# Attention's transfers between tiles issued from GpSimd's queue, in a two-layer decoder trunk on one core

## The chip, the cores and the metric

The kernel runs on one core of a Trainium2 chip. The metric is device microseconds of one execution. The engines are named as in the profile: PE is TensorE, PEld its weight loads, DVE VectorE, ACT ScalarE, POOL GpSimd, SP SyncE. Each of them works through its own list of instructions in order, and a transfer (DMA) is issued by an instruction in the list of one of them.

## The reference

The program computes a trunk of two layers for 512 tokens of width 1024, ahead of which 16 learned tokens are put (528 in all). Layer 0 is attention with a forget gate, layer 1 a gated linear recurrence; each is followed by a gated MLP with a short convolution. The change lies in the attention:

```
xn = rms_norm(h, norm_g)
q, k, v, f_logit, o_gate = split(xn @ w_in)            # 16 heads of 64
q = rms_norm(q, q_gain) * hd ** -0.5;  k = rms_norm(k, k_gain)
c = cumsum(log_sigmoid(f_logit + b_f))                 # per head
s = q . k + c[query] - c[key], -inf above the diagonal
o = softmax(s) @ v
h = h + (o * sigmoid(o_gate)) @ w_out
```

## The kernel before, in words

The whole trunk is one program, a chain of stages: setup, attention (`fox`), MLP, recurrence (`hgrn`), MLP. Activations lie transposed, 128 channels by 528 tokens, and are worked on in two halves of 264. Matrix products are computed to near float32 by splitting each operand into a high and a low part (`xhi`/`xlo`, `hi`/`lo`) and adding three products: these are the lines L263, L266 and L267, the projections, and L312 for the values. Weights come from DRAM by SP's queue into `raw`; ACT rounds them to `hi` (L210) and DVE makes `lo` (L126).

Attention goes by eight pairs of heads `p` in a software pipeline. One step of the loop runs for different pairs at once:

- `stage_a(p+3)`: the projections of q and k (L263 to L267), their squares on ACT (L545) and the scaled copy (L546). A product with `hsel` (L554) gives the sums of squares in `strow`; four transfers (L559) lay them out as `am2`, DVE takes the inverse root, and two transfers (L569) bring it back as `rows`.
- `stage_n(p+2)`: a product with `rows` (L583) spreads the factors over the partitions, DVE multiplies (L584), ACT rounds to `stg` (L588), and `pack` sends the high and low parts by six transfers per pair (L610) into `pk`, the operand tiles of one head. There are six such tiles, `pk_245` to `pk_270`, used in turn.
- `stage_l(p+1)`: four transfers per pair (L619) put the forget gate's cumulative sums `cneg` into the operand tile. Then `lse` finds the logarithm of each query's sum of exponentials for each head: scores by L726, L727 and, on the diagonal, L729; DVE reduces to the maximum `negm` (L739, L745); ACT takes exponentials with their sum (L119, to `junk`, with an accumulator read) and a logarithm (`ls`); DVE splits it (`lr`, L757, L126); a transposition by TensorE (L760) and a DVE copy (L762) give the row `lrow`, and three transfers (L765, L766) write it into the operand tile.
- `stage_t(p)`: `attend` computes the scores again, transposed and now with that row in the contraction (L782, L783; mask L785), ACT takes exponentials `pt` (L119), and L797 multiplies with the values.

The output projection at the end reads tiles that were operands before (`pk_265`, `pk_270` as its high and low part). The first MLP's weights are partly formed by transfers that add: SP brings one summand, POOL issues a transfer that accumulates the other (L232).

The pieces are written in an order that `weave` sets by costs in the code, and the program is then scheduled by the tile framework, which simulates a timeline and from that sets the order of each engine's list:

```
        for p in range(-3, NPAIR):
            ...
            weave(
                (chain(*fill), 0.97 * cost),
                (stage_n(p + 2) if 0 <= p + 2 < NPAIR else None, 1.0),
                (stage_l(p + 1) if 0 <= p + 1 < NPAIR else None, 4.3),
                (stage_t(p) if p >= 0 else None, 8.5),
                (stage_f() if p == -2 else None, 3.5),
            )
```

Which engine issues a transfer is chosen in the code; where it stands in that engine's list, and in which order TensorE takes projections and scores, follows from the simulated timeline. PSUM has two banks for projections (`psp`), four for scores (`pss`), one for attention's output (`psc`) and one for sums and factors (`psd`).

Of the kernel before, what the change touches and what calls it, by code (L numbers as in the profile page):

```python
# [12 lines left out]
F32 = mybir.dt.float32  # L13
# [69 lines left out]
class Builder:  # L83
# [297 lines left out]
    def fox(self, ctx):  # L381
        nc, tc, a = self.nc, self.tc, self.a
# [38 lines left out]
        def bank():  # L421
            return self.bank("p")
# [96 lines left out]
        def stage_a(p):  # L519

            raw = {}
            sqs = []
            blocks = []
            for w_ in range(2):
                wt = self.weights(a["wqk"][p, w_], KT) if p else self.first[w_]
                banks = [self.bank(b) for b in ("pp", "cd")[w_]] if p == 0 else None
                blocks.append((wt, banks))
                if p == 0 and w_ == 1:
                    units = [
                        self.proj_unit(ps[:, :tn], [wt], self.x, t0, tn)  # L530
                        for wt, banks in blocks
                        for ps, (t0, tn) in zip(banks, full)
                    ]
                    for step in zip(*units):
                        yield sum(step)
            for w_, nm in ((0, "q"), (1, "k")):
                wt, banks = blocks[w_]
                sq = (s2 if w_ else self.sqp).tile([P, T], F32, name="sqq", tag="sqk" if w_ else "sq", bufs=2 - w_)
                rw = s2.tile([P, T], F32, name="raw" + nm, tag="raw" + nm)
                g = qg if nm == "q" else self.vcol(V_KG)  # L540
                for i, (t0, tn) in enumerate(full):
                    ps = banks[i] if banks else bank()
                    if not banks:
                        yield from self.proj_unit(ps[:, :tn], [wt], self.x, t0, tn)
                    nc.scalar.square(sq[:, t0 : t0 + tn], ps[:, :tn])  # L545
                    nc.scalar.activation(rw[:, t0 : t0 + tn], ps[:, :tn], AF.Copy, scale=g)  # L546
                sqs.append(sq)
                raw[nm] = rw

            strow = s2.tile([P, 264], F32, name="strow", tag="strow", bufs=1)  # L550
            pst = self.bank("d")
            for g in range(4):
                t0, tn = full[g % 2]
                mm(pst[32 * g : 32 * g + 32, :tn], hsel, sqs[g // 2][:, t0 : t0 + tn], start=True, stop=True)  # L554
            nc.scalar.copy(strow, pst[:, :264])
            yield 0.9
            am2 = self.tiny.tile([64, 33], F32, name="am2", tag="am2")
            for g in range(4):
                nc.sync.dma_start(  # L559
                    am2[16 * g : 16 * g + 16, :], strow[32 * g : 32 * g + 2, :].rearrange("r (j c) -> r j c", c=33)  # L560
                )
            nc.vector.tensor_tensor(am2, am2, et, ALU.add)
            y = self.rsqrt(am2, "q")
            yr = self.tiny.tile([64, 2, 33], F32R, name="yr", tag="yr")
            nc.vector.tensor_copy(yr[:, 0, :], y)
            self.sub(yr[:, 1, :], y, yr[:, 0, :].bitcast(F32))
            rows = rowbufs[p % 2]
            for x in range(2):
                nc.sync.dma_start(  # L569
                    rows[8 * x : 8 * x + 8, :].rearrange("r (j c) -> r j c", c=33).bitcast(F32),  # L570
                    yr[:, x, :].bitcast(F32),
                )
            scaled[p] = raw, rows
# [29 lines left out]
        def pack(p, stg):  # L603
            packs[p] = []
            for hd in range(2):
                head = 2 * p + hd
                d = slots[head % NSLOT]
                packs[p].append(d)
                sl = slice(64 * hd, 64 * hd + 64)
                dma = lambda o, i: nc.sync.dma_start(o.bitcast(F32), i.bitcast(F32))  # L610
                dma(d["pk"][0:64, 0:2, :], stg[sl, 0:3:2, :])
                dma(d["pk"][0:64, 2:4, :], stg[sl, 0:4:3, :])
                dma(d["pk"][64:128, 2:4, :], stg[sl, 1:3, :])

        def stage_l(p):
            for hd, d in enumerate(packs[p]):
                head = 2 * p + hd
                for x in range(2):
                    nc.sync.dma_start(  # L619
                        d["k1"][64 + x : 65 + x, :].rearrange("x (j c) -> x j c", c=CW).bitcast(F32),  # L620
                        cneg[8 * head : 8 * head + 8, x, :].bitcast(F32),
                    )
            for d in packs[p]:
                yield from self.lse(d, s2, identb, maskq)
# [42 lines left out]
        for p in range(-3, NPAIR):  # L667
# [4 lines left out]
            if p + 3 < NPAIR:  # L672
                fill.append(stage_a(p + 3))
                cost += 12.8
# [6 lines left out]
            if p == NPAIR - 1:  # L681
# [3 lines left out]
# [5 lines that stand above are left out]
# [4 lines left out]
            while gated and p >= max(gated[0], 5 + gated[0] // 4):  # L694
                m = gated.pop(0)
                o = gate[:, m, :]
# [15 lines left out]
    def lse(self, d, s2, identb, maskq):  # L712

        nc = self.nc
        mm = nc.tensor.matmul
        q1, k1, q2, k2 = d["q1"], d["k1"], d["q2"], d["k2"]
        negm = self.tiny.tile([P, 6], F32, name="negm", tag="negm")
        ssum = self.tiny.tile([P, 6], F32, name="ssum", tag="ssum")
        nc.gpsimd.memset(negm, 0.0)
        nc.gpsimd.memset(ssum, 1.0)  # L720

        def score(i, qs, qn, c0, c1):
            ps = self.bank("s")
            o = ps[:qn, : c1 - c0]
            diag = c1 > qs
            mm(o, q1[0:66, qs : qs + qn], k1[0:66, c0:c1], start=True, stop=False)  # L726
            mm(o, q2[:, qs : qs + qn], k2[:, c0:c1], start=False, stop=not diag)  # L727
            if diag:
                mm(ps[:qn, qs - c0 : qs - c0 + qn], identb[:qn, :qn], maskq[:qn, :qn], start=False, stop=True)  # L729
            return o  # L730

        def expsum(o, qn, col, src):
            junk = s2.tile([P, 400], BF16, name="junk", tag="junk")
            self.act(junk[:qn, : o.shape[1]], o, AF.Exp, bias=negm[:qn, col : col + 1], accum_out=ssum[:qn, src : src + 1])

        for i in range(4):
            qs, qn = QT[i]
            o = score(i, qs, qn, 0, qs + qn)
            nc.vector.tensor_reduce(negm[:qn, i : i + 1], o, AX.X, ALU.max, negate=True)  # L739
            expsum(o, qn, i, i)  # L740
            yield 0.3
        qs, qn = QT[4]
        oa = score(4, qs, qn, 0, 264)
        ob = score(4, qs, qn, 264, 528)
        nc.vector.tensor_reduce(negm[:, 4:5], oa, AX.X, ALU.max, negate=True)  # L745
        nc.vector.tensor_reduce(negm[:, 5:6], ob, AX.X, ALU.max, negate=True)
        nc.vector.tensor_tensor(negm[:, 4:5], negm[:, 4:5], negm[:, 5:6], ALU.min)
        expsum(oa, qn, 4, 4)
        expsum(ob, qn, 4, 5)
        yield 0.6  # L750
        nc.vector.tensor_tensor(ssum[:, 4:5], ssum[:, 4:5], ssum[:, 5:6], ALU.add)
        ls = self.tiny.tile([P, 5], F32, name="ls", tag="ls")
        self.act(ls, ssum[:, 0:5], AF.Ln)
        self.sub(ls, negm[:, 0:5], ls)

        lr = self.tiny.tile([P, 10], F32R, name="lr", tag="lr")
        nc.vector.tensor_copy(lr[:, 0:5], ls)  # L757
        self.sub(lr[:, 5:10], ls, lr[:, 0:5].bitcast(F32))
        pr = self.bank("s")
        mm(pr[:10, :P], lr, self.identr, start=True, stop=True)  # L760
        lrow = self.tiny.tile([10, P], F32R, name="lrow", tag="lrow")
        nc.vector.tensor_copy(lrow, pr[:10, :P])  # L762
        for x in range(2):
            row = q1[96 + x : 97 + x, 16:].rearrange("x (i c) -> x i c", c=P)
            nc.sync.dma_start(row.bitcast(F32), lrow[5 * x + 1 : 5 * x + 5, :].bitcast(F32))  # L765
        nc.sync.dma_start(q1[96:98, 0:16].bitcast(F32), lrow[0:10:5, 0:16].bitcast(F32))  # L766
        yield 0.2

    def attend(self, o0, o1, p, ds, v, po, s2, maskk):
# [763 lines left out]
```

## Time and profile before

| | |
|---|---|
| median of 3 runs | 1461.14 us (1461.13 to 1461.83) |
| the profiled execution's own time | 1463.9 us |
| its span | 1462.0 us |
| mean granted clock of TensorE | 0.994 |
| TensorE busy | 1435.2 us, 98% |
| VectorE, ScalarE, GpSimd busy | 67%, 45%, 10% |
| transfers | 230.97 MB, mean 158 GB/s |

In the profile, "PE psp L263 <- ACT xhi L332" means that a matmul of line 263 into a tile psp waited for ScalarE's write of xhi at line 332. In an instruction's row, the first number is its start from the beginning of the span, the second its duration; a bracket holds how long the engine was idle before it and what ended that. Matmuls are pipelined, so a row's duration is longer than the step from one to the next.

### The profile page before, as it was taken

To read this page: it belongs to the slowest core of one execution; us is meant where nothing else is said; L and a number is where in the kernel's file an instruction comes from. 1 tells how busy PE (TensorE), PEld (TensorE's weight loads), DVE (VectorE), ACT (ScalarE), POOL (GpSimd) and SP (SyncE) were. 2 spreads that over 40 slices of the span, in tenths; PEclk is the share of its full clock that TensorE was granted. 3 is DMA by queue.
4 is the path that set the end of the run, shared out by engine and by line. 5 is a ranking of instruction groups with operands and counts; after the bars stand their busy time and mean duration, and the time that the engine had idled before them with its cause. 6 is when DMAs were issued, how large, how long until landed. Compare 5 with 4: busy or idle time off the path is not lost.

```text
span 1462.0 us, 29172 instructions
## 1 busy us (share of the span) xinstructions
PE 1435.2 (98%) x11482; PEld 1349.0 (92%) x11482; DVE 974.9 (67%) x2079; ACT 663.1 (45%) x1293; POOL 150.2 (10%) x265
## 2 busy tenths in 40 slices
PE   7999999999999999999999999999999999999998
PEld 6888888888999999999999999999999889999997
DVE  6555555774667675666785667587567777866773
ACT  5355555563434444333563224333345565544551
POOL 6000000001112100112001101011111110000000
PEclk9999999999999999999999999999999999999999
DMA  4433334435999884678737617374587795544542
GB/s 160 119 105 90 90 90 123 124 99 137 293 231 247 213 254 137 171 193 197 218 92 181 168 22 181 91 178 103 126 238 169 208 265 162 173 143 137 161 146 85
DMA packets 99696, 230.97 MB, mean 158 GB/s; under 512 B 13528, under 2 KB 15320, under 8 KB 99560
## 3 DMA queue, kind: packets, MB, share of 16 engines
q1 hardware_dynamic: 79400, 188.47, 40.3%
q0 software_dynamic: 20160, 40.64, 18.3%
q8 instruction: 90, 1.47, 0.4%
q14 instruction: 46, 0.38, 0.1%
HBM read 213.62 MB, written 75.24 MB: 198 GB/s over the span
## 4 chain that ended last, share of the span: by engine, by line
PE 91%; DMA 4%; DVE 2%; ACT 1%; issue 1%; SPq 1%; ACTq 0%; DVEq 0%
PE psp L263 9%; PE psp L267 9%; PE psp L266 9%; PE pss L263 8%; PE pss L267 8%; PE pss L266 8%; PE psp L312 5%; PE psc L797 2%; PE psp L1292 2%; PE psp L1290 2%; PE psp L1291 2%; PE psp L1184 1%; PE psp L1186 1%; PE psp L1185 1%; PE pss L951 1%; PE psd L1292 1%
## 5 line engine op out<-in xcount | busy, mean ns | idle before, releaser
L210 ACT CAST hi<-raw 128x1024 fp32r<-128x1024 f32 (+3 forms) x250 | 234.1, 939 | 381.3 <-PE psp L266 96.1
L126 DVE TENSOR_TENSOR lo<-raw,hi 128x1024 fp32r<-128x1024 f32 (+3 forms) x254 | 275.5, 1088 | 100.9 <-ACT hi L210 96.8
L263 PE MATMUL psp<-xhi,hi 128*128 128x264 f32 (+1 forms) x984 | 283.9, 290 | 6.1 <-ACT xhi L332 6.1
L266 PE MATMUL psp<-xlo,hi 128*128 128x264 f32 (+1 forms) x984 | 283.6, 288 | 3.2 <-DVE xlo L333 3.2
L267 PE MATMUL psp<-xhi,lo 128*128 128x264 f32 (+1 forms) x984 | 283.9, 289 | 0.0
L263 PEld LDWEIGHTS psp<-xhi,hi 128*128 128x128 f32 x984 | 186.8, 190 | 10.7 <-ACT xhi L332 6.1
L266 PEld LDWEIGHTS psp<-xlo,hi 128*128 128x128 f32 x984 | 187.1, 190 | 6.0 <-DVE xlo L333 3.7
L267 PEld LDWEIGHTS psp<-xhi,lo 128*128 128x128 f32 x984 | 187.0, 190 | 1.7 <-issue 1.6
L267 PE MATMUL pss<-xhi,lo 128*128 128x264 f32 (+3 forms) x520 | 149.8, 288 | 0.0
L263 PE MATMUL pss<-xhi,hi 128*128 128x264 f32 (+3 forms) x520 | 149.1, 287 | 0.0
L266 PE MATMUL pss<-xlo,hi 128*128 128x264 f32 (+3 forms) x520 | 149.1, 287 | 0.0
L232 POOL DMA_DIRECT2D s<-gu x80 | 66.4, 856 | 332.3 <-DMA s<-gu 300.9
L263 PEld LDWEIGHTS pss<-xhi,hi 128*128 128x128 f32 x520 | 97.8, 188 | 0.6
L267 PEld LDWEIGHTS pss<-xhi,lo 128*128 128x128 f32 x520 | 97.7, 188 | 0.7
L266 PEld LDWEIGHTS pss<-xlo,hi 128*128 128x128 f32 x520 | 97.7, 188 | 0.7
L263 PE MATMUL pss<-room,hi 128*128 128x512 f32 (+1 forms) x182 | 69.6, 387 | 1.7 <-ACT hi L210 1.7
L267 PE MATMUL pss<-room,lo 128*128 128x512 f32 (+1 forms) x182 | 70.4, 387 | 0.0
L266 PE MATMUL pss<-room,hi 128*128 128x512 f32 (+1 forms) x182 | 70.2, 386 | 0.0
L312 PE MATMUL psp<-hi,xhi 128*128 128x256 f32 x232 | 66.9, 288 | 2.5 <-ACT v L599 2.5
L1292 PE MATMUL psp<-xhi,lo 128*128 128x258 f32 x240 | 67.9, 283 | 0.9 <-DVE lo L126 0.8
L1157 ACT CAST hi<-left 128x768 fp32r<-128x768 f32 (+1 forms) x56 | 43.4, 781 | 54.0 <-PE psp L1185 18.3
L1290 PE MATMUL psp<-xhi,hi 128*128 128x258 f32 x240 | 67.6, 282 | 0.0
(488 smaller groups left out, 3798.1 us busy)
## 6 DMA issues: line engine op xcount, KB each, us to landing
raw<-gu SPq DMA_DIRECT2D x48, 512.0 KB
s<-gu SPq DMA_DIRECT2D x80, 256.0 KB
s<-gu POOLq DMA_DIRECT2D x80, 256.0 KB, 6.0
raw<-gu SPq DMA_DIRECT2D x60, 256.0 KB
pk<-stg SPq DMA_DIRECT2D x48, 264.0 KB
raw<-s SPq DMA_DIRECT2D x40, 256.0 KB
raw<-s SPq DMA_DIRECT2D x20, 512.0 KB
raw<-wqk SPq DMA_DIRECT2D x14, 512.0 KB
```

The costliest lines, as they stand in the source:

```text
L126: self.nc.vector.tensor_tensor(out, x, y, ALU.subtract)
L210: nc.scalar.copy(hi, raw)
L232: nc.gpsimd.dma_start(out, y, accum_op=ALU.add, max_dma_last_dim=4 * n)
L263: ins = mm(ps, hi[:, i, :], xh, start=k == 0, stop=False)
L266: mm(ps, hi[:, i, :], xl, start=False, stop=False)
L267: mm(ps, lo[:, i, :], xh, start=False, stop=k == total - 1)
L312: mm(ps[:tn, :256], y[:, t0 : t0 + tn], w, start=n == 0, stop=n == 23)
L797: ins = mm(o, v[:kn, j, 2 * (p % 2) + hd, :], w[hd][0], start=j == 0, stop=j == last)
L1157: nc.scalar.copy(hi, raw)
L1290: mm(ps, hi[:, k0 + k, :], xh, start=start and k == 0, stop=False, skip_group_check=not start)
L1291: mm(ps, hi[:, k0 + k, :], xl, start=False, stop=False, skip_group_check=not start)
L1292: mm(ps, lo[:, k0 + k, :], xh, start=False, stop=k == 3, skip_group_check=not start)
```

## The change

176 transfers of the attention are issued by GpSimd in place of SP: 32 of `am2` (L559), 16 of `rows` (L569), 48 of `pk` from `stg` (L610), 32 of `cneg` (L619) and 48 of `lrow` (L765, L766). The loads of weights, of the gate's `z` and of the residual stay on SP. The two memsets in `lse`, 32 in all, go from GpSimd to VectorE. Nothing is added or removed.

```diff
--- before.py
+++ after.py
@@ -556,7 +556,7 @@
             yield 0.9
             am2 = self.tiny.tile([64, 33], F32, name="am2", tag="am2")
             for g in range(4):
-                nc.sync.dma_start(
+                nc.gpsimd.dma_start(
                     am2[16 * g : 16 * g + 16, :], strow[32 * g : 32 * g + 2, :].rearrange("r (j c) -> r j c", c=33)
                 )
             nc.vector.tensor_tensor(am2, am2, et, ALU.add)
@@ -566,7 +566,7 @@
             self.sub(yr[:, 1, :], y, yr[:, 0, :].bitcast(F32))
             rows = rowbufs[p % 2]
             for x in range(2):
-                nc.sync.dma_start(
+                nc.gpsimd.dma_start(
                     rows[8 * x : 8 * x + 8, :].rearrange("r (j c) -> r j c", c=33).bitcast(F32),
                     yr[:, x, :].bitcast(F32),
                 )
@@ -607,7 +607,7 @@
                 d = slots[head % NSLOT]
                 packs[p].append(d)
                 sl = slice(64 * hd, 64 * hd + 64)
-                dma = lambda o, i: nc.sync.dma_start(o.bitcast(F32), i.bitcast(F32))
+                dma = lambda o, i: nc.gpsimd.dma_start(o.bitcast(F32), i.bitcast(F32))
                 dma(d["pk"][0:64, 0:2, :], stg[sl, 0:3:2, :])
                 dma(d["pk"][0:64, 2:4, :], stg[sl, 0:4:3, :])
                 dma(d["pk"][64:128, 2:4, :], stg[sl, 1:3, :])
@@ -616,7 +616,7 @@
             for hd, d in enumerate(packs[p]):
                 head = 2 * p + hd
                 for x in range(2):
-                    nc.sync.dma_start(
+                    nc.gpsimd.dma_start(
                         d["k1"][64 + x : 65 + x, :].rearrange("x (j c) -> x j c", c=CW).bitcast(F32),
                         cneg[8 * head : 8 * head + 8, x, :].bitcast(F32),
                     )
@@ -716,8 +716,8 @@
         q1, k1, q2, k2 = d["q1"], d["k1"], d["q2"], d["k2"]
         negm = self.tiny.tile([P, 6], F32, name="negm", tag="negm")
         ssum = self.tiny.tile([P, 6], F32, name="ssum", tag="ssum")
-        nc.gpsimd.memset(negm, 0.0)
-        nc.gpsimd.memset(ssum, 1.0)
+        nc.vector.memset(negm, 0.0)
+        nc.vector.memset(ssum, 1.0)
 
         def score(i, qs, qn, c0, c1):
             ps = self.bank("s")
@@ -762,8 +762,8 @@
         nc.vector.tensor_copy(lrow, pr[:10, :P])
         for x in range(2):
             row = q1[96 + x : 97 + x, 16:].rearrange("x (i c) -> x i c", c=P)
-            nc.sync.dma_start(row.bitcast(F32), lrow[5 * x + 1 : 5 * x + 5, :].bitcast(F32))
-        nc.sync.dma_start(q1[96:98, 0:16].bitcast(F32), lrow[0:10:5, 0:16].bitcast(F32))
+            nc.gpsimd.dma_start(row.bitcast(F32), lrow[5 * x + 1 : 5 * x + 5, :].bitcast(F32))
+        nc.gpsimd.dma_start(q1[96:98, 0:16].bitcast(F32), lrow[0:10:5, 0:16].bitcast(F32))
         yield 0.2
 
     def attend(self, o0, o1, p, ds, v, po, s2, maskk):
```

With other costs in the simulated timeline the scheduler writes the lists of the attention stage in another order; behind that stage they are as before. Three places follow.

The first is TensorE's list at the first pair of heads (`pk_245` holds head 0, `pk_250` head 1; `psp` rows are projections, `pss` rows with `pk` scores). TensorE's list before, round the first head's L760:

```order
L263 MATMUL psp<-xhi,hi 128x264
L266 MATMUL psp<-xlo,hi 128x264
L583 MATMUL psd<-rows_177,selr 128x264
L267 MATMUL psp<-xhi,lo 128x264
L263 MATMUL psp<-xhi,hi 128x264
L760 MATMUL pss<-identr,lr 10x128
L726 MATMUL pss<-pk_250 16x16
L727 MATMUL pss<-pk_250 16x16
```

TensorE's list after, from the last scores of head 0 to the first of head 1:

```order
L726 MATMUL pss<-pk_245 128x264
L727 MATMUL pss<-pk_245 128x264
L726 MATMUL pss<-pk_245 128x264
L727 MATMUL pss<-pk_245 128x264
L729 LDWEIGHTS identb
L729 MATMUL pss<-maskq,identb 128x128
L760 MATMUL pss<-identr,lr 10x128
L726 MATMUL pss<-pk_250 16x16
```

and further on in the same list, from the last scores of head 1:

```order
L729 LDWEIGHTS identb
L729 MATMUL pss<-maskq,identb 128x128
L760 MATMUL pss<-identr,lr 10x128
L583 MATMUL psd<-rows_177,selr 128x264 x4
L554 MATMUL psd<-sqq,hsel 32x264 x4
L263 MATMUL psp<-xhi,hi 128x264
```

Before, projections stand among the scores of these heads and round L760; now the scores of head 0, its L760, the scores of head 1, its L760, the L583 and the L554 stand in direct succession, and projections follow.

The transfers of the same place, SP's list before and GpSimd's now (`rows_177` is one of two buffers of `rows`). SP's list before:

```order
L207 DMA raw<-wv 128x1024
L619 DMA pk_245<-cneg 1x8x66 x2
L569 DMA rows_177<-yr 8x8x33 x2
L619 DMA pk_250<-cneg 1x8x66 x2
L619 DMA pk_255<-cneg 1x8x66 x2
L619 DMA pk_260<-cneg 1x8x66 x2
L207 DMA raw<-wv 128x1024
L619 DMA pk_265<-cneg 1x8x66 x2
L619 DMA pk_270<-cneg 1x8x66 x2
L765 DMA pk_245<-lrow 1x4x128 x2
L766 DMA pk_245<-lrow 2x16
```

GpSimd's list after, at the first two heads' lrow:

```order
L619 DMA pk_260<-cneg 1x8x66
L619 DMA pk_265<-cneg 1x8x66
L619 DMA pk_270<-cneg 1x8x66
L765 DMA pk_245<-lrow 1x4x128 x2
L766 DMA pk_245<-lrow 2x16
L569 DMA rows_177<-yr 8x8x33 x2
L765 DMA pk_250<-lrow 1x4x128 x2
L766 DMA pk_250<-lrow 2x16
```

On SP the rows stood ahead of the cneg of the heads and of the first lrow, among loads of weights; on GpSimd they stand between the lrow of head 0 and that of head 1, and no load of weights is among them.

The second place is TensorE's list at a later pair (the tiles are in their second use; `pk_245` and `pk_250` are being attended while `pk_260` begins `lse`). TensorE's list before:

```order
L263 MATMUL psp<-xhi,hi 128x264
L266 MATMUL psp<-xlo,hi 128x264
L267 MATMUL psp<-xhi,lo 128x264
L263 MATMUL psp<-xhi,hi 128x264
L797 MATMUL psc<-pt,v_185 64x256
L760 MATMUL pss<-identr,lr 10x128
L797 MATMUL psc<-pt,v_185 64x256
L797 MATMUL psc<-pt,v_185 64x128 x2
L726 MATMUL pss<-pk_260 16x16
```

TensorE's list after, at the same head's L760:

```order
L782 MATMUL pss<-pk_245 128x256
L783 MATMUL pss<-pk_245 128x256
L782 MATMUL pss<-pk_250 128x256
L783 MATMUL pss<-pk_250 128x256
L782 MATMUL pss<-pk_245 128x128
L783 MATMUL pss<-pk_245 128x128
L782 MATMUL pss<-pk_250 128x128
L783 MATMUL pss<-pk_250 128x128
L760 MATMUL pss<-identr,lr 10x128
L726 MATMUL pss<-pk_260 16x16
L727 MATMUL pss<-pk_260 16x16
```

Before, projections and products with the values stand round the transposition L760; now scores of attended heads, L760 and the scores of the next head follow one another. A like place lies some 450 rows ahead of it, and another near the stage's end.

The third is the end of the stage, from the last L760, behind which the last head's lrow is sent, to the first score that reads it (`pk_260`). TensorE's list before, up to that score:

```order
L263 MATMUL psp<-pk_265,hi 128x264
L266 MATMUL psp<-pk_270,hi 128x264
L267 MATMUL psp<-pk_265,lo 128x264
L263 MATMUL psp<-pk_265,hi 128x264
L266 MATMUL psp<-pk_270,hi 128x264
L267 MATMUL psp<-pk_265,lo 128x264
L782 MATMUL pss<-pk_260 128x256
L783 MATMUL pss<-pk_260 128x256
```

TensorE's list after, the same place:

```order
L267 MATMUL psp<-pk_265,lo 128x264
L760 MATMUL pss<-identr,lr 10x128
L782 MATMUL pss<-pk_255 128x256
L783 MATMUL pss<-pk_255 128x256
L782 MATMUL pss<-pk_260 128x256
L783 MATMUL pss<-pk_260 128x256
L263 MATMUL psp<-pk_265,hi 128x264
```

Before, the L760 stands nine rows further ahead, followed by the two scores of `pk_255` and twelve projection matmuls, of which the last six are shown; now only the two scores of `pk_255` stand between L760 and the first score of `pk_260`.

## The prediction, made before the changed kernel was run

> **What bounds the kernel now.** I read the page's first part, then the waits of TensorE, then short windows round the attention stage, and last single instructions there. The first part gives the bound:
>
> ```profile
> span 1462.0 us, 29172 instructions
> PE 1435.2 (98%) x11482; PEld 1349.0 (92%) x11482; DVE 974.9 (67%) x2079; ACT 663.1 (45%) x1293; POOL 150.2 (10%) x265
> ```
>
> TensorE is busy 98% of the span, so only time in which it stands still or runs slowly can come back, and there is little. In the list of waits (what waited <- on what: us in total, times, longest) these lie in the attention stage, which ends near 345 us:
>
> ```profile
> PE psp L312 <- ACT v L599: 2.5, 2, 1.3
> PE pss L782 <- DMA pk<-lrow: 1.9, 1, 1.9
> PE pss L726 <- DMA pk<-cneg: 1.2, 1, 1.2
> PE pss L782 <- ACT junk L119: 0.9, 1, 0.9
> PE psd L583 <- DMA rows<-yr: 0.8, 1, 0.8
> PE pss L782 <- ACT pt L119: 0.6, 1, 0.6
> ```
>
> Three of the six are transfers that this change moves: 1.9 + 1.2 + 0.8 = 3.9 us. That is the most that faster transfers can give directly. The windows (stretch, its length, then PE, weight loads, DVE, ACT and POOL busy with counts, granted clock, DMA share, GB/s) give the pitch and the clock:
>
> ```profile
> 75.00:100.00 25.00, 25.00 (x197) 22.14 (x197) 12.00 (x35) 13.33 (x41) 0.43 (x4) 0.94 0.39 93
> 294.00:304.00 10.00, 10.00 (x76) 8.30 (x76) 8.34 (x22) 7.31 (x20) 0.23 (x2) 1.00 0.37 93
> 325.00:350.00 25.00, 21.63 (x143) 18.64 (x143) 13.50 (x37) 11.03 (x31) 1.77 (x2) 0.86 0.43 106
> ```
>
> At full clock a matmul takes 10.00/76 = 0.13 us. ACT is busy 7.31 us in those ten, DVE 8.34: neither is far from TensorE, and attention's own work runs on them only because projections stand between. Where TensorE had waited, the clock granted afterwards is lower (0.86, 0.94). Single matmuls show the step; columns are start, modelled duration, engine, line:
>
> ```profile
> 331.11 0.42 PE L263 MATMUL psp<-pk,hi 128*128 128x264 f32 x1
> 331.33 0.42 PE L266 MATMUL psp<-pk,hi 128*128 128x264 f32 x1
> 334.22 0.29 PE L263 MATMUL psp<-pk,hi 128*128 128x264 f32 x1
> 334.34 0.28 PE L266 MATMUL psp<-pk,hi 128*128 128x264 f32 x1
> 335.75 0.22 PE L760 MATMUL pss<-identr,lr 128*10 128x128 f32 x1
> 339.62 0.36 PE L782 MATMUL pss<-pk 98*128 98x256 f32 x1 [1.91 <-DMA pk<-lrow]
> ```
>
> The pitch is 0.22 us behind a wait and 0.12 us about 3.4 us later, so a dip costs some 1.7 us. The chain of waits names the same transfers, with their time from issue to landing:
>
> ```profile
> 138.19 3.60 DMA rows<-yr
> 337.90 1.59 DMA pk<-lrow
> ```
>
> **The change, part by part.** 176 transfers go from SP's queue to POOL's: 32 am2, 16 rows, 48 pk<-stg, 32 cneg, 48 lrow. Their price, and POOL's other work:
>
> ```profile
> L765 SPq DMA_DIRECT2D pk<-lrow x32: 573/611/697, 86.3 to 337.3; - x32
> L232 POOL DMA_DIRECT2D s<-dn x32: 814/814/1446, 328.1 to 509.0; - x32
> DMA to landing us min/median/max: 3.8/6.1/12.0
> POOL ssum L720 <- ACT ls L119: 256.3, 14, 48.9
> L359 DVE MEMSET am<- x4: 59/59/59, 0.9 to 401.4; 128x1 f32 x4
> ```
>
> SP is relieved of 176 x 0.61 = 107 us of issuing in some 290 us. That returns nothing by itself: no wait above is on a weight's transfer. POOL gains 176 x 0.81 = 143 us, half of the same 290 us, in order. No row shows POOL issuing a small transfer inside the chip; its price lies between SP's 0.61 and the longest 1.45 of the accumulating L232, and I take the median 0.81, which is also the minimum there. Landing lies between 1.59 and the 6.1 of 256 KB accumulations; I take 1.7, near the row of the same 2 KB transfer. The Trainium skill ("DMA: Bandwidth & Descriptors", section on the anatomy of a DMA on the SWDGE, or gpsimd, path) fits 2.0 us plus bytes/436e3 for a GpSimd transfer, so 2.0 us here, an estimate; no row of this case has one so small from POOL; by it the sum below would be 0.6 higher.
>
> The 32 memsets of 0.059 us cost VectorE 1.9 us, hidden beside its 33% idle time. They had to move: on POOL they wait 256 us in all for the Ln of an earlier head, and every transfer behind them in that queue would wait too. Now POOL's waits are for the transfers' own sources. An lrow waits for its cast (L762), and behind it stand the next pair's rows, so a late lrow makes those late; L583 waits for them.
>
> The am2, pk<-stg and, but for its first, the cneg transfers I cost at nothing: nobody on TensorE waits for the first two in the list above, because each pair's are sent while the projections of a later pair run. A pair has 22 transfers, 17.9 us at 0.81, in the 36 us that a pair takes (290/8). If that cover were gone, the six pk<-stg of a pair would come 6 x 0.63 + 4.4 = 8.2 us later, which is in the rival of slow transfers.
>
> What costs time is the order. The order written for TensorE has changed all through the attention stage: at five places scores of two heads stand back to back without the projections that stood between them (three are quoted with the change). TensorE then goes at the pace of this chain (groups in attention; line, engine, operation, count | busy, mean ns | idle before), first ACT, then DVE:
>
> ```profile
> L119 ACT ACTIVATE junk<-pss,negm 16x16 bf16<-16x16 f32 (+2 forms) x96 | 42.3, 443 | 29.0 <-DVE negm L739 16.3 <-DVE rqq L347 4.0 <-DVE ruq L346 3.8
> L119 ACT ACTIVATE pt<-pss 128x272 f32<-128x272 f32 (+4 forms) x103 | 32.3, 331 | 38.7 <-DVE pss L785 21.9 <-PE pss L783 15.8
> L210 ACT CAST hi<-raw 128x1024 fp32r<-128x1024 f32 (+1 forms) x28 | 27.2, 971 | 32.4 <-PE psp L266 21.6 <-DMA raw<-wqk 8.1 <-DMA raw<-wg 2.0
> L119 ACT ACTIVATION_READ_ACCUMULATOR junk<-pss,negm 128x1 f32 (+1 forms) x96 | 18.7, 195 | 0.0
> L545 ACT ACTIVATE sqq<-psp 128x264 f32<-128x264 f32 x23 | 9.0, 389 | 4.7 <-PE psp L267 4.7
> L588 ACT CAST stg<-rawk 128x528 fp32r<-128x528 f32 x7 | 4.4, 633 | 2.1 <-DVE rawk L584 2.1
> L119 ACT ACTIVATE ls<-ssum 128x5 f32<-128x5 f32 x16 | 3.5, 216 | 1.8 <-DVE ssum L751 1.8
> ```
>
> ```profile
> L739 DVE TENSOR_REDUCE negm<-pss 16x1 f32<-16x16 f32 (+1 forms) x64 | 23.0, 365 | 9.5 <-PE pss L729 8.9
> L745 DVE TENSOR_REDUCE negm<-pss 128x1 f32<-128x264 f32 x16 | 6.8, 428 | 11.1 <-PE pss L727 11.1
> L584 DVE TENSOR_TENSOR rawk<-rawk,psd 128x264 f32<-128x264 f32 x14 | 6.0, 427 | 6.9 <-PE psd L583 6.8
> L762 DVE CAST lrow<-pss 10x128 fp32r<-10x128 f32 x16 | 4.4, 274 | 1.7 <-PE pss L760 1.6
> 73.06 0.16 DVE L739 TENSOR_REDUCE negm<-pss 16x1 f32<-16x16 f32 x1 [0.18 <-PE pss L729]
> 83.55 0.16 DVE L126 TENSOR_TENSOR ls<-negm,ls 128x5 f32<-128x5 f32 x1
> 83.95 0.16 DVE L126 TENSOR_TENSOR lr<-ls,lr 128x5 fp32r<-128x5 f32 x1
> ```
>
> The two rows are the waits that stood ahead of and at the first place before:
>
> ```profile
> 52.73 0.39 PE L312 MATMUL psp<-hi,xhi 128*128 128x256 f32 x1 [1.25 <-ACT v L599]
> 72.56 0.17 PE L726 MATMUL pss<-pk 66*16 66x16 f32 x1 [1.18 <-DMA pk<-cneg]
> ```
>
> *A, the first pair of heads.* Now the scores of head 0, its L760, the scores of head 1, its L760, four L583 and four L554 follow one another. From first score to L760 a head needs four reduces and two, 4 x 0.365 + 2 x 0.43 = 2.3; the two exps of the last tile with their accumulators, 2 x (0.443 + 0.195) = 1.3 (the earlier ones run beside the reduces); minimum and sum, 0.4; Ln 0.2; three small steps from 83.55 at 0.2 each, 0.6; with six hand-overs of 0.18 to 0.2 (the row at 73.06), 1.2, that is 6.0 us. Two heads take 12.0. The rows on POOL follow three lrow and come 0.3 + 5 x 0.81 + 0.27 + 1.7, about 6.4 us, behind the first L760: 0.4 beyond the second. Four L583 follow, each behind the L584 before it, since the bank must be free: 0.43 and two hand-overs of 0.2, 4 x 0.83 = 3.3; four L554 of two passes, 8 x 0.13 = 1.0. Together 16.7, in which 48 matmuls x 0.13 = 6.2 are work. 10.5 lost, less what was waited for there before (1.25 and 1.18 in these rows): **+8.1**. Bounds: 5.7 with hand-overs for nothing; with POOL at 1.45 and 6.1 the rows are 5 x 0.63 + 4.4 = 7.6 later.
>
> *B, two packed stretches later.* Each has some 74 matmuls, 9.6 us, while ACT must do ten score exps with accumulators (6.4), ten pt (3.3), one hi (1.0), L545 and L546 (0.4, 0.5), one stg (0.6), one Ln (0.2): 12.4. 2.8 each, 5.6, less the 1.3 of L599 and the 0.8 of rows that were waited for: **+3.5**. Bounds: 0 if ACT enters them ahead; twice that if the chain is served no better than in A.
>
> *C, the last such stretch:* 64 matmuls in the same way, 2.5, less 0.6 + 0.9: **+1.0**; bounds -1.5 and 2.5.
>
> *D, the end.* Before, twelve projection matmuls stand between the last L760 and the first score that needs its lrow, and 1.9 us are still waited. Now four stand there. From L760 the transfer needs 0.9 to the first issue, 3 x 0.81 to issue and 1.7 to land, 5.0; less four matmuls, 0.4, it is 4.6, against 1.9: **+2.7**. One L232 accumulation stands ahead of these lrow in POOL's order; I take it as issued by then, as the first was at 328.1. Bounds: -1.9, if projections bridge it after all, and 3 x 0.63 + 4.4 = 6.3 more at 1.45 and 6.1.
>
> *E, the clock.* A and one of the later stalls last long enough to be followed by a dip as at 331; two more at 1.7: **+3.4**; bounds 0 and 6.8.
>
> Sum: 8.1 + 3.5 + 1.0 + 2.7 + 3.4 = 18.7. The profiled execution's own time is 1463.9, 2.8 above the median 1461.1; it would become 1482.6, the median 1479.8, say **1480**.
>
> **The rivals.** *Bridged:* ACT and DVE enter the packed stretches ahead, so that only A at its lower bound and D remain: 5.7 + 2.7, 1469.5. For it speaks ACT's 45%; against it that each score needs DVE's answer before ACT can begin.
>
> *Slow POOL transfers:* issuing at 1.45 and landing at 6.1 as its accumulations do: 7.6 more at A, 6.3 at D, 1494. Against it speaks that 0.81 is both median and minimum of L232 while VectorE is 67% busy; those are large transfers from DRAM, so it stays open. The Trainium skill ("SBUF — State Buffer", section "🔬 SBUF: two separate sides") says that VectorE's two-port operations keep GpSimd from writing descriptors, which would make these transfers late; a median equal to the minimum in a busy stage speaks against it here.
>
> *Faster:* with two queues no transfer stands behind another kind's. Gone would be 2.5 + 1.2 + 0.8 + 1.9 = 6.4 of waits and two dips, 3.4: 1451.3. It decides if the packed stretches together cost less than 9.8, for which A alone would have to be mostly covered; the hand-overs speak against that.
>
> *No change within 0.2%* (2.9 us, about what a measurement can tell): gains of this size just eaten by A, 1461.
>
> **How the numbers follow.** Forecast 0.58 (its own range 1472 to 1489, from A, B and E at their bounds), slow POOL 0.18, bridged 0.14, faster 0.06, no change 0.04. So faster 0.06, same 0.04, slower 0.90. The range begins at 1465.0 (A at 5.7, D's 1.9 gone) and ends at 1498 (slow POOL and two more dips, 1497).
>
> **What would show it.** After A's place, TensorE's waits on negm, ls and lr near 70 to 90 us, some 10 us in all, with a window's PE busy time below 16 of 25; a wait of L782 for pk<-lrow of 4 to 5 us near the end; POOL's issues near 0.81 each; granted clock below 0.9 after these. Wrong would be: no such waits (then bridged), or waits on pk<-stg, rows and am of over 3 us each in every pair (then slow POOL), or a stage shorter than 345 us.

## The result, and the profile after

| | before | after |
|---|---|---|
| median of 4 runs | 1461.14 us (1455.57 to 1461.83) | 1508.42 us (1507.04 to 1509.37) |
| ratio to before | | 1.0332, interval 1.0314 to 1.0350 |
| the profiled execution's own time, span | 1463.9, 1462.0 us | 1507.96, 1506.2 us |
| mean granted clock | 0.994 | 0.975 |

The change costs 47 us. The forecast was 1480, with a range up to 1498: the sign was right, the size was not. The first part of the page of the changed kernel:

```profile
span 1506.2 us, 29159 instructions
PE 1452.9 (96%) x11482; PEld 1361.6 (90%) x11482; DVE 973.9 (65%) x2111; ACT 665.5 (44%) x1293; POOL 244.1 (16%) x409
```

The same 11482 matmuls are busy 17.7 us longer, though nothing was added; this goes with the lower clock. The rest is mostly waits. TensorE's waits in the changed kernel (only those that are new or larger):

```profile
PE pss L727 <- DMA pk<-stg: 7.3, 2, 6.3
PE pss L726 <- DMA pk<-stg: 5.7, 1, 5.7
PE pss L782 <- DMA pk<-lrow: 4.2, 1, 4.2
PE pss L760 <- DVE ruq L345: 3.0, 1, 3.0
PE pss L782 <- ACT junk L119: 3.0, 5, 1.3
PE pss L760 <- DVE lr L126: 3.0, 1, 3.0
PE psp L312 <- ACT v L599: 3.0, 1, 3.0
```

The largest, 13.0 us for pk<-stg, is one that the prediction priced at nothing. The waits of L760 and those for junk are the packed stretches. Where they lie, in windows of the changed kernel (PE, weight loads, DVE, ACT, POOL busy with counts, granted clock, DMA share, GB/s):

```profile
75.00:100.00 25.00, 15.62 (x84) 12.08 (x83) 12.20 (x48) 10.19 (x34) 9.99 (x19) 0.66 0.09 17
150.00:175.00 25.00, 21.80 (x125) 15.88 (x125) 13.82 (x59) 13.98 (x48) 6.47 (x12) 0.80 0.07 13
225.00:250.00 25.00, 21.96 (x130) 16.14 (x129) 14.00 (x58) 13.40 (x46) 5.57 (x11) 0.80 0.03 7
250.00:275.00 25.00, 22.05 (x171) 19.40 (x170) 8.35 (x33) 9.29 (x26) 6.74 (x13) 0.93 0.45 126
350.00:375.00 25.00, 17.69 (x86) 13.32 (x87) 9.82 (x32) 10.12 (x38) 3.07 (x5) 0.60 0.39 86
```

In each, TensorE gets through 84 to 171 matmuls where some 195 were usual. No engine is full there; in the first, none is busy for more than 16 of the 25 us, and the engines wait for one another. For a sum by place I took, for every matmul up to 425 us, the step to the next one less the median step of the same line and shape before the change:

| us from the start | loss before | loss after | difference |
|---|---|---|---|
| 0 to 50 | 10.8 | 9.8 | -1.0 |
| 50 to 100 (the first pair) | 8.6 | 17.1 | +8.5 |
| 100 to 225 | 11.6 | 18.4 | +6.8 (5.3 of it from 150 to 175) |
| 225 to 275 | 4.7 | 16.6 | +11.9 |
| 275 to 325 | 1.3 | 1.0 | -0.3 |
| 325 to 425 (the last pair and the end) | 7.6 | 27.8 | +20.2 |
| sum | 44.6 | 90.8 | +46.2 |

Of the 46.2, 28 are recorded waits (39.4 after, 11.2 before); 18 are slower steps behind and between them. The two spans differ by 44.2 us, so behind 425 us the changed kernel lost 2 us less. Single instructions at the first pair (84 and 91 us) and at the last:

```profile
84.32 0.26 PE L760 MATMUL pss<-identr,lr 128*10 128x128 f32 x1 [3.05 <-DVE ruq L345]
91.21 0.27 PE L760 MATMUL pss<-identr,lr 128*10 128x128 f32 x1 [2.97 <-DVE lr L126]
350.25 1.17 PE L726 MATMUL pss<-pk 66*16 66x16 f32 x4 [5.65 <-DMA pk<-stg]
357.67 0.20 PE L727 MATMUL pss<-pk 128*16 128x16 f32 x1 [6.25 <-DMA pk<-stg]
384.94 0.58 PE L782 MATMUL pss<-pk 98*128 98x256 f32 x1 [4.16 <-DMA pk<-lrow]
```

The two L760 are 6.9 us apart: one head's chain in the packed first pair, which the prediction put at 6.0. The last pair's operands came late because they were sent late. From all instructions of L610, on SP before and on POOL after (first and last start stand behind the durations):

```profile
L610 SPq DMA_DIRECT2D pk<-stg x48: 550/700/1827, 57.1 to 291.6; - x48
```

```profile
L610 POOL DMA_DIRECT2D pk<-stg x48: 512/607/648, 63.6 to 350.5; - x48
DMA to landing us min/median/max: 3.1/5.5/9.2
```

The last of them starts 59 us later, while TensorE had lost only 26 more by 325 us. In the order of TensorE's list the last pair's L583, which stand ahead of these transfers, moved towards the end: the work between each pair's last L583 and its first score, summed with each shape at its mean step before the change and without waits, was 16, 11, 9, 12, 13, 15, 22 and 23 us before, and is 17, 5, 7, 6, 10, 8, 8 and 3 us now. The last 3 us cannot cover six issues and a landing.

### The profile page after: what moved, and what is told of

Read it like the earlier page. It is cut to its first block, busy times and chain, and to the rows that moved or that the text cites. A ratio compares the mean times of both kernels' runs of the same rounds, so it can differ in the third digit from the quotient of the medians.

```text
span 1506.2 us, 29159 instructions
## 1 busy us (share of the span) xinstructions
PE 1452.9 (96%) x11482; PEld 1361.6 (90%) x11482; DVE 973.9 (65%) x2111; ACT 665.5 (44%) x1293; POOL 244.1 (16%) x409
## 4 chain that ended last, share of the span: by engine, by line
PE 87%; DMA 4%; issue 4%; DVE 2%; ACT 1%; POOL 1%; SPq 0%; ACTq 0%; DVEq 0%; POOLq 0%
PE psp L263 8%; PE psp L266 8%; PE psp L267 8%; PE pss L263 8%; PE pss L267 8%; PE pss L266 8%; PE psp L312 5%; PE psp L1292 2%; PE psp L1291 2%; PE psp L1290 2%; PE psc L797 2%; DMA pk<-stg 1%; PE psp L1184 1%; PE psp L1186 1%; PE psp L1185 1%
## 5 line engine op out<-in xcount | busy, mean ns | idle before, releaser
L1291 PE MATMUL psp<-xlo,hi 128*128 128x258 f32 x240 | 67.6, 282 | 0.0
```

The source lines that it names most:

```text
L1291: mm(ps, hi[:, k0 + k, :], xl, start=False, stop=False, skip_group_check=not start)
```

## The experiments

Two theories stood against each other. *Order*: the loss is in the lists that the scheduler wrote for the new queue. *Queue*: GpSimd's queue itself makes transfers late. To tell them apart, lists were held: `fix_order` adds, for each list given, an ordering edge without a wait from every instruction to the next one in it, so the scheduler can write no other.

```diff
     with tile.TileContext(nc, schedule_with_timeline_sim=True) as tc:
         trace(tc, a)
+        fix_order(tc)
```

Ratios are to the kernel before, with 95% intervals.

**1. New queues, TensorE's old list.**

> All 176 transfers on GpSimd and the memsets on VectorE, as changed, but TensorE's list held in the order that it had before the change. Theory 'order' (the loss is TensorE's new order; the transfers themselves are no slower than SP's): the packed stretches and the two waits for pk<-stg of about 6 us go, since some 23 us of TensorE's work again stand between the last pair's L583 and its first score; 1450 to 1465 us. Theory 'queue' (GpSimd's transfers come late: pk<-stg lands 5.5 us in the median and up to 9.2 behind its issue, and a waiting transfer holds up those behind it): the waits stay in another place, 1485 us or more.

1488.14 us, 1.0195 (1.0170 to 1.0220): between the two. The packed stretches are gone; one wait is new:

```profile
PE psd L583 <- DMA rows<-yr: 16.4, 8, 4.7
```

**2. Old queues, TensorE's new list.**

> All transfers on SP and the memsets on GpSimd, as before the change, but TensorE's list held in the order of the changed kernel. Theory 'order': the packed stretches stay at their price and the last pair's pk<-stg is waited for again; 1490 to 1512 us. Theory 'queue': transfers on SP are in time in either order; 1461 to 1475 us.

1518.75 us, 1.0410 (1.0384 to 1.0436), 10 us slower than with the new queues. So TensorE's new list costs no less without any transfer on GpSimd (the lists of the other engines were written anew here too). Its waits:

```profile
PE pss L760 <- DVE lr L126: 20.4, 5, 8.3
PE pss L726 <- DMA pk<-stg: 5.4, 1, 5.4
PE pss L782 <- DMA pk<-lrow: 4.0, 1, 4.0
PE pss L727 <- DMA pk<-stg: 2.7, 1, 2.7
```

With every transfer on SP the last pair's pk<-stg is still waited for 8.0 us (11.9 in the changed kernel), and the last lrow 4.0 (4.2 there). These two waits come with TensorE's order; GpSimd's queue is not needed for them. SP's timeline ahead of L760's longest wait, at the first pair:

```profile
72.85 5.63 SPq L619 DMA_DIRECT2D pk<-cneg  x8
79.00 1.46 SPq L569 DMA_DIRECT2D rows<-yr  x2
80.56 0.38 SPq L207 DMA_DIRECT2D raw<-wv  x1
```

A load of weights is issued only behind eight cneg and two rows. On ScalarE its rounding stands ahead of the last two exps of the head, and they wait with it:

```profile
84.15 1.04 ACT L210 CAST hi<-raw 128x1024 fp32r<-128x1024 f32 x1 [4.13 <-DMA raw<-wv]
```

**3. The new list up to the seventh pair, the rest in the old order.**

> Queues as changed; TensorE's list follows the changed kernel up to the L554 of the seventh pair (some 215 us in) and takes what is left in the order of before. It divides the loss by place. By the excess over the nominal pitch, the changed kernel lost 43.1 us from 225 us on against 13.5 before. Theory 'order': that difference of 30 us goes and the loss of the first 225 us stays, 1474 to 1486 us. Theory 'queue': the last pair's transfers stay late, 1495 us or more.

1502.60 us, 1.0301 (1.0273 to 1.0329): neither range. The 12 us for pk<-stg at the last pair went (1.8 is left), but 7.3 us of waits for rows came in two places, as in the first run. An old list for TensorE, whole as in run 1 or in part as here, takes away only some of the loss while the other lists are new.

**4. Transfers moved, memsets left on GpSimd.**

> The 176 transfers on GpSimd, the 32 memsets left there too. TensorE's order has the same packed first pair, and 4.9 us of work between the last pair's L583 and its first score (3.3 in the changed kernel). The prediction held that the memsets, waiting for an earlier head's Ln, would hold up the transfers behind them: then lrow and rows come later and the time is above the changed kernel's, 1512 to 1530. If a memset's wait is always over before its transfer's source is ready, 1500 to 1511.

1501.77 us, 1.0286 (1.0259 to 1.0312), a little less than the changed kernel. GpSimd's memsets still wait, as one row shows:

```profile
POOL ssum L720 <- ACT ls L119: 116.0, 12, 14.3
```

So the transfers can move to GpSimd without the memsets, other than the prediction held. What these 116 us cost by themselves stays open: TensorE's list differs too, with 4.9 us of work ahead of the last pair's first score in place of 3.3, and the waits for pk<-stg come to 5.5 us in place of 13.0.

**5. TensorE's, VectorE's and ScalarE's lists held.**

> As the first experiment (all 176 transfers on GpSimd, TensorE's list as before the change), with VectorE's and ScalarE's lists also held as before. There TensorE waited 16.4 us in 8 waits for rows, and the first step on the way to rows on VectorE (L562) began 0 to 7 us, 2.9 in the mean, behind the landing of am2. Theory 'landing' (am2 lands late on GpSimd's queue, behind the 264 KB pk<-stg): the waits stay at 10 us or more, 1476 to 1488 us. Theory 'list' (VectorE's new list sets L562 too late): the waits go below 4 us, 1460 to 1470.

1472.94 us, 1.0089 (1.0065 to 1.0114). The waits for rows fall from 16.4 to 2.2, though am2 land as before. VectorE's timeline at the same pair, in run 1 and here:

```profile
177.02 0.18 DVE L562 TENSOR_TENSOR am<-am,et 64x33 f32<-64x33 f32 x1
```

```profile
167.50 0.19 DVE L562 TENSOR_TENSOR am<-am,et 64x33 f32<-64x33 f32 x1 [2.47 <-DMA am<-strow]
```

In run 1 L562 begins without a wait, 7.0 us behind the last landing at 170.0: other work of VectorE stood ahead of it in its list. Here VectorE waits for the transfer and goes on at once, 0.2 us behind the landing at 167.3. That is the theory 'list', though the time is 3 us above its range. What remains in TensorE's waits of this run are a first cneg and small ones:

```profile
PE pss L726 <- DMA pk<-cneg: 4.8, 1, 4.8
PE pss L782 <- DMA pk<-lrow: 3.0, 1, 3.0
PE psd L583 <- DMA rows<-yr: 2.2, 2, 1.6
```

**6 and 7. As run 1, with am2 or pk<-stg back on SP.** In `stage_a` (L559), and in `pack`:

```diff
-                nc.gpsimd.dma_start(
+                nc.sync.dma_start(
                     am2[16 * g : 16 * g + 16, :], ...
```

```diff
-                dma = lambda o, i: nc.gpsimd.dma_start(...)
+                dma = lambda o, i: nc.sync.dma_start(...)
```

> As the first experiment, with the 32 am2 transfers back on SP. Theory 'landing': am2 no longer stands behind pk<-stg, which cost it 4 to 5 us of landing, and rows are in time: waits for rows below 5 us, 1460 to 1470 us. Theory 'list' or 'POOL is slow for every small transfer': waits for rows stay above 8 us, 1476 to 1490.

> As the first experiment, with the 48 pk<-stg back on SP and the small transfers on GpSimd. Theory 'landing': with no large transfer ahead of them all am2 land as the first four do, about 1.8 us behind their issue (6 to 7 us there), waits for rows below 5 us, 1460 to 1470 us. Theory 'POOL is slow for every small transfer': am2 keep landing after 4 us or more and the waits stay above 8 us, 1476 to 1490.

1473.89 (1.0095, 1.0075 to 1.0115) and 1469.18 us (1.0068, 1.0049 to 1.0086). Both are below run 1, and waits for rows are 4.2 us or less, but the reason given, am2 landing late behind pk<-stg in one queue, does not hold: with pk<-stg on SP am2 still land after 4.8 us in the median (5.7 in run 1). What changed is again VectorE's list, which was free: in run 1 it waits for am2 once, for 0.5 us, in run 6 eight times, so L562 is no longer set late there. L562's wait before and in run 6:

```profile
  DMA am<-strow: 15.4, 8
```

```profile
  DMA am<-strow: 25.1, 8
```

With am2 on SP and pk<-stg on GpSimd (run 6), L562 begins 2.4 to 6.1 us behind the last am2's issue in the seven pairs that have pk<-stg under way, and 1.8 in the first, which has none. Before, with both on SP, it was 1.7 to 1.8 in all eight. So another queue does not bring a small transfer past the large ones. The Trainium skill ("DMA: Bandwidth & Descriptors", section "🔬 Queues, rings and completion order") says that a transfer's signal lands only after every earlier write of that DMA engine, across its queues; runs 6 and 7 agree.

**8. The changed kernel with am2 on SP, lists free.**

> As the changed kernel, with am2 back on SP and no list held. The order now has 17 to 34 us of TensorE's work between each pair's L583 and its first score (4 to 17 in the changed kernel), and no packed first pair. Theory 'landing': what made the order bad and the transfers late was am2's way; 1455 to 1470 us. Theory 'queue': moving the rest is what costs; 1480 or more.

1475.10 us, 1.0097 (1.0062 to 1.0132): between the theories; two thirds of the loss go with a fifth of the transfers.

**9. All lists held, the moved transfers in SP's old order among themselves.**

> As the fifth experiment (176 transfers on GpSimd; TensorE's, VectorE's and ScalarE's lists as before the change), with the 176 also held in the order in which they stood among themselves on SP, and SP's own loads in theirs. Nothing is left of the change but the queue. There the first pair's cneg was waited for 4.8 us, since others stood ahead of it. Theory 'list' (queue harmless in an unchanged order): 1458 to 1466 us, the wait for cneg at 2 us or less. Theory 'queue' (transfers collide with weights that SP now issues earlier, GpSimd begins later after a signal): 1468 to 1477 us.

1463.75 us, 1.0022 (1.0009 to 1.0035). In its trace TensorE's, VectorE's and ScalarE's instructions, the 176 transfers and SP's loads stand in the order of before. This is the price of the queue in the old lists: about 3 us (1.3 to 5.1) of 47. The counterpart, all of the new lists with the transfers on SP, was not run. The first pair's cneg is back at its old wait; what is left is the end, and rows:

```profile
PE pss L782 <- DMA pk<-lrow: 3.0, 1, 3.0
PE psd L583 <- DMA rows<-yr: 2.0, 2, 1.5
PE pss L726 <- DMA pk<-cneg: 1.3, 1, 1.3
```

**10. The kernel before, with 14 projection matmuls moved ahead of the first score.**

> The kernel before, queues and lists as they were, but 14 projection matmuls (1.8 us) taken ahead of the first pair's first score, which waited 1.18 us for cneg and was followed by a stretch at a granted clock of 0.94 (1.5 us in 25). If a wait is worth what it leaves behind too: 2 to 4 us faster, 1456 to 1459 beside 1460.6. If the wait comes back at the next hand-over of that pair (its L760 now has less projection work ahead): no change, within 1 us.

1466.82 us, 1.0046 (1.0029 to 1.0063), slower. The wait for cneg went, and another, of 4.8 us, took its place. ScalarE's timeline shows why:

```profile
PE psp L312 <- ACT v L599: 6.3, 2, 4.8
```

```profile
107.56 1.04 ACT L210 CAST hi<-raw 128x1024 fp32r<-128x1024 f32 x1 [7.15 <-DMA raw<-wqk]
```

SP's list was not held as it was: three lrow transfers now stand ahead of the last am2 and of two loads of wqk. ScalarE waits for such a load, and `v` stands behind it in its list. So this run does not tell what the wait for cneg was worth.

**11 to 18. Some groups moved, lists free.** Each is the change's own line for the groups named, with the memsets on VectorE; the others stay on SP.

> Only the 32 cneg transfers on GpSimd (and the memsets on VectorE), lists free. The order has 16 to 35 us of TensorE's work between each pair's L583 and its first score and no packed stretch. Theory 'list': 1454 to 1466 us. Theory 'queue' (any transfer on GpSimd costs): 1468 or more.

> Only the 48 pk<-stg transfers on GpSimd (and the memsets on VectorE), lists free. The order has 11 to 30 us of TensorE's work between each pair's L583 and its first score and no packed stretch. Theory 'list': 1454 to 1466 us. Theory 'queue' (264 KB transfers on GpSimd beside SP's weights make both late): 1468 or more.

> Only am2 and rows (48 transfers) on GpSimd, memsets on VectorE, lists free. Theory 'feedback path' (these two stand between L554 and L583 of every pair, so their assumed lateness is what reorders TensorE): 7 to 17 us of work between L583 and the first score, 8 us from first score to L760 at the first two heads (12 and 10 before); 1464 to 1478 us. Theory 'sum' (no group alone does it): 1456 to 1463.

> Only the 32 am2 on GpSimd, memsets on VectorE, lists free. Half of the feedback path; the order also puts the last head's first score only two matmuls behind L760, as in the changed kernel. Theory 'feedback path': 1463 to 1474 us. Theory 'sum': 1456 to 1462.

> pk<-stg and cneg (80 transfers) on GpSimd, memsets on VectorE, lists free; am2, rows and lrow on SP. 20 to 39 us of work between L583 and the first score. The end has two matmuls between the last L760 and the score that reads its lrow, which on SP was worth 1.9 us of wait with twelve. Theory 'feedback path': near before, with 2 us for the end, 1458 to 1465 us. Theory 'sum': 80 of 176 moved transfers bring a proportional part of the loss, 1470 or more.

> As the changed kernel, but am2 and rows back on SP; lists free. 18 to 33 us of work between L583 and the first score, no packed first pair, the end as in the changed kernel. Theory 'feedback path': 1460 to 1468 us. Theory 'sum': 128 of 176 transfers moved, 1480 or more.

> pk<-stg, am2 and rows (96 transfers) on GpSimd, memsets on VectorE, lists free; cneg and lrow on SP. Either group alone cost nothing (0.9988 and 0.9998 of before). Theory 'shared queue' (the loss arises where am2 and rows share GpSimd's queue with the 264 KB pk<-stg): the order has three stretches of 10 us with 2 to 4 us of projections, as the changed kernel has, and 5 to 14 us between L583 and the first score; 1480 to 1500 us. Theory 'sum': what the groups cost alone, 1456 to 1465.

> As the changed kernel, but pk<-stg back on SP, lists free: the 128 small transfers share GpSimd's queue. The order has a packed first pair (5.2 and 2.0 us from first score to L760) and 4 to 14 us between L583 and the first score, but on SP pk<-stg needs less of it. Theory 'shared queue': without the large transfers the loss is mostly gone, 1463 to 1478 us. Theory 'sum' by count: 128 of 176, 1485 or more.

| run | on GpSimd | transfers | us | ratio (interval) |
|---|---|---|---|---|
| 11 | cneg | 32 | 1459.97 | 1.0000 (0.9985 to 1.0015) |
| 12 | pk<-stg | 48 | 1458.01 | 0.9988 (0.9974 to 1.0003) |
| 13 | am2, rows | 48 | 1460.70 | 0.9998 (0.9979 to 1.0016) |
| 14 | am2 | 32 | 1463.53 | 1.0021 (1.0009 to 1.0033) |
| 15 | pk<-stg, cneg | 80 | 1471.55 | 1.0071 (1.0049 to 1.0092) |
| 16 | pk<-stg, cneg, lrow | 128 | 1468.51 | 1.0055 (1.0035 to 1.0076) |
| 17 | pk<-stg, am2, rows | 96 | 1486.60 | 1.0189 (1.0156 to 1.0222) |
| 18 | all but pk<-stg | 128 | 1476.66 | 1.0102 (1.0071 to 1.0134) |
| the change | all | 176 | 1508.42 | 1.0332 (1.0314 to 1.0350) |

Runs 13 and 14 refute 'feedback path' as the sole cause: am2 and rows together cost nothing, am2 alone 0.2%. Runs 16 and 17 refute the plain 'sum': 128 transfers cost 0.6%, 96 others 1.9%. Run 15 lies in the range of 'sum', above 1470, but at 0.7% where 80 of 176 would be 1.5%. Pk<-stg costs nothing alone, am2 with rows nothing alone, both together 1.9%, as 'shared queue' expected in 17 and 18. Sharing the queue is not enough, though: in run 9 all 176 share it and cost 0.2%. That leaves the lists that the scheduler writes when these groups share GpSimd's queue. The waits of run 17 are of many kinds, none large:

```profile
PE psp L312 <- ACT v L599: 4.4, 1, 4.4
PE pss L782 <- DMA pk<-lrow: 3.9, 1, 3.9
PE pss L727 <- DMA pk<-stg: 3.8, 3, 1.6
PE pss L726 <- DMA pk<-cneg: 3.7, 1, 3.7
```

In runs 15 and 16 the largest part of the cost is the end, where lists of such kernels put the last head's score two matmuls behind its L760: the loss from 325 to 350 us is 11.1 and 11.9 us, 6.8 before. No run beats the kernel before clearly; pk<-stg alone on GpSimd comes nearest, its interval reaching above 1. Why the scheduler writes worse lists then, by which of its assumptions, no run here shows.

## Why the prediction was wrong, point by point

- *Bound, and the place of the loss.* Right: all of it lies in the attention stage, as waits of TensorE and as lower clock behind them, and no list changed behind that stage.
- *The transfers that I cost at nothing.* This step failed. The am2 and pk<-stg were priced at zero "because each pair's are sent while the projections of a later pair run", by the waits of the old list. For the last pair the new list had taken that cover, 23 us down to 3. The prediction named the price of a lost cover (8.2 us a pair) and gave it to the rival of slow transfers; it was the list, and it cost 11.9 us of waits at two matmuls, 8.0 with the transfers on SP (run 2). It stood in the order: packed scores were priced, the distance from a producer to its reader was not.
- *A.* Right in mechanism and near in size: 8.1 forecast, 9.8 with one of E's dips, and 8.5 measured with its dip. Each head took 6.9 us (6.0 forecast); rows were not waited for.
- *B.* Right in mechanism, too small: 3.5 forecast, 5.3 (150 to 175 us) + 6.3 (225 to 245 us) = 11.6 measured, dips included. TensorE's waits there come to 3.2 and 3.0 us; the rest is pace. Another 5.5 us went from 245 to 275 us, outside a packed stretch: a wait of 2.95 us for v (L599) and its dip, where the sum had taken such waits as gone.
- *C.* 1.0 forecast. Its stretch is the one with the 11.9 us for pk<-stg; from 345 to 372 us TensorE lost 18.5 us, 12.2 of them in waits.
- *D.* The wait for lrow was forecast at 4.6, and was 4.16. The parts were off and offset each other: two matmuls stand there, not four, the three issues took 1.5 us, not 2.4, and the last landed some 2.5 us behind its issue, not 1.7. With the transfers on SP and the same list the wait was 4.0 (run 2).
- *E.* This step failed too, by its size. Two more dips of 1.7, 3.4 us, were forecast from dips behind single waits; slower steps cost 18. Before, the granted clock was 0.50 for three stretches of 3.41 us in this stage; after, for 17.1, 10.2, 10.2 and 23.9 us at the packed stretches. One dip before, and two windows of the changed kernel:

```profile
330.57:333.98 3.41, 3.41 (x17) 3.41 (x18) 2.40 (x8) 0.81 (x6) 0.00 (x0) 0.50 0.53 100
```

```profile
156.90:165.10 8.20, 8.20 (x33) 5.93 (x34) 2.45 (x8) 3.87 (x13) 2.76 (x5) 0.50 0.02 3
346.05:369.94 23.89, 13.18 (x59) 10.57 (x60) 10.91 (x31) 9.49 (x32) 6.29 (x11) 0.50 0.58 135
```

  From 156.9 to 165.1 us TensorE has no recorded idle time, and the clock stays at 0.50. What differs from the dip before is the work: 33 matmuls in 8.2 us against 17 in 3.4, and weight loads busy for 5.9 of 8.2 us against all of 3.4. Whether this keeps the clock low, no run shows. The Trainium skill ("TensorE: Matmul & The Clock Gate", section "HAM oscillation — how this bites in real kernels") warns of idle gaps above about 3.4 us; at the first pair the longest gap was 3.05 us and the clock still fell to 0.66 over the window. So shorter gaps are not safe here.
- *POOL's price.* Too high for the issue and right for a landing alone: 0.51 to 0.65 us for pk<-stg, 0.61 in the median, against 0.81 assumed and SP's median of 0.70; lrow lands 1.5 us behind its issue at best, 1.8 in the median for L766, against 1.7 assumed. With 264 KB under way small transfers take up to 9 us, which the rival of slow transfers had nearer.
- *Rivals.* 'Slow POOL transfers' gave 1494 by landing times; the time was on its side, but run 9 shows that the queue's own part is about 3 us. 'Bridged' and 'no change' failed: A alone cost 8.5. 'Faster' failed: in run 9 the separate queue took away no wait for a transfer (lrow 3.0 in place of 1.9, rows 2.0 in place of 0.8, cneg 1.3 in place of 1.2).

## What to carry to other kernels

Where a scheduler sets the lists, a change of queue is a change of every engine's list: compare the lists for the distance from each producer to its reader, at every pair and not only where rows look crowded, and price a cover in the new list. To part the two effects, hold the lists and change the queue; holding one engine's list alone misleads, since the other lists are written for another timing. Here a packed stretch cost its waits and a half clock for 10 to 24 us. A faster issue is not an earlier landing: measure from the first issue to the reader.

## What the runs showed of the hardware that was not expected

GpSimd issued these transfers faster than SP (medians 0.61 against 0.70 us for pk<-stg, 0.50 against 0.62 for L766), yet they did not land sooner. A pair's six pk<-stg, its am2 and L562, which waits for them, before and in run 9:

```profile
57.10 6.11 SPq L610 DMA_DIRECT2D pk<-stg  x6
63.31 3.70 SPq L559 DMA_DIRECT2D am<-strow  x4
68.20 0.19 DVE L562 TENSOR_TENSOR am<-am,et 64x33 f32<-64x33 f32 x1 [3.11 <-DMA am<-strow]
```

```profile
57.88 3.43 POOL L610 DMA_DIRECT2D pk<-stg  x6 [14.53 <-ACT stg L588]
61.30 2.34 POOL L559 DMA_DIRECT2D am<-strow  x4
68.83 0.19 DVE L562 TENSOR_TENSOR am<-am,et 64x33 f32<-64x33 f32 x1 [3.23 <-DMA am<-strow]
```

SP takes 6.1 us to issue the six and GpSimd 3.4, but from the first issue to L562 it is 11.1 us in the one and 10.95 in the other: what SP spends in issuing, the transfers from GpSimd spend between issue and landing.

A transfer of some 2 KB landed 1.5 us behind its issue when alone, and am2 landed after 5.7 us in the median with the 264 KB transfers on the same queue (run 1), 4.8 with them on the other (run 7).
